# Spilled gates stored by groups of four keys, and stored from the SyncE queue

## The chip, the cores and the metric

The kernel runs on one core of a Trainium2 chip. The metric is the device time of one execution in microseconds (us). The kernel before was timed three times: 1623.45, 1630.87 and 1631.17 us, a median of 1630.87 us. One more execution was profiled.

## The reference, cut to what matters

The program is one decoder block over 512 tokens of width 1024: three gated token mixers, then a product-key expert retrieval ("PEER"). Only the second part matters here. Each token picks 16 of 128 x 128 = 16384 experts for each of 8 heads, 128 (expert, gate) pairs in all, and computes

```python
a   = einsum('cd,ced->ce', h_c, u[e_c])
act = gelu(a) * g_c
out = einsum('ce,ced->cd', act, v[e_c])
```

An expert's number is `e1 * 128 + e2`; the first key `e1` splits the tables u and v into 128 blocks of 128 experts, and the kernel calls the number of such a block a key, `k`.

## The kernel before, in words

The 512 tokens are four blocks of 128. For blocks 0 and 1 the kernel gathers each picked row of u and v from memory by an indirect DMA issued by GpSimd (line 833, tile `row`, 512 KB each): a dot product on VectorE for u (line 843, tile `scr`), a scaled sum on VectorE for v (line 852, tile `mg`). At most five such rows have a buffer, some more for a while, and at most `AHEAD` = 4 are requested ahead of the one in use. `step()` does one row, and JOBS lists all 512 of them.

For blocks 2 and 3 (`DENSE`, `ND` = 2 blocks, `TD` = 256 tokens) it computes all experts densely. For each key k it multiplies 128 expert rows of u with the 256 tokens (`dense_u`, line 971 in full float32, or lines 142 to 144 as three products of split operands), applies gelu, multiplies by a matrix of gates that is zero for the experts not picked, and multiplies with 128 rows of v, summing over keys in four PSUM banks (`dense_v`, lines 142 to 144). One key's activations `ga` are 128 experts x 256 tokens.

The gate matrix is made in the *spread* stage. Its loop over n takes four tokens at a time (`GT` = 4): VectorE builds one-hot sides `o` (line 1026), ScalarE scales one by the gates (line 1029), TensorE multiplies them (line 1041), and the product holds, for the 128 second keys in the partitions, four tokens x 128 first keys. The gates of the first 32 keys (`KEPT`) are multiplied at once into `ga` by VectorE (line 1044). Those of the other 96 keys are copied by ScalarE into three staging tiles `st` (line 1047), each for `SPILT` = 32 keys x `TG` = 32 tokens; the staging tiles take turns with two sets of buffers. When 32 tokens are full, three DMAs (line 1051) write them to the memory tensors `gd`, one for each dense block. There are 8 such groups of tokens, so 24 DMAs of 512 KB, all on ScalarE's DMA queue.

The *last* stage is the loop over k at line 1173. `operands(k)` asks for the v block of key k + 3 on SyncE's queue (`fetch_v`, line 1073, tiles `raw` and `last`), and every fourth key asks for the gates of the next four (`GK` = 4) keys in two DMAs of 256 KB on the same queue (`get_gates`, line 1065, tile `gq`), 48 in all. Then ScalarE splits v into `whi` (line 1090) and the activations into `ah` (line 1088), VectorE makes the remainders `wlo` (line 128) and `al` (line 1093), and multiplies gates in (line 1085). Between these it does the rows of `step()`. The blocks of u still to do (71 of 128) come on ScalarE's queue there (line 935), every second one is split by ScalarE and VectorE into `uhi` and `ulo` (lines 958 and 960).

The order on TensorE, VectorE and GpSimd is the program's order (a manual schedule). ScalarE's and SyncE's instructions are placed by a scheduler that simulates time, with some SyncE issues held in program order. Each engine takes its instructions in order, and a DMA issue that waits holds up what stands behind it on its engine.

Of the kernel before, what the change touches and what calls it, by code (L numbers as in the profile page):

```python
# [7 lines left out]
F32 = mybir.dt.float32  # L8
# [13 lines left out]
NK = 128  # L22
# [5 lines left out]
ND = len(DENSE)  # L28
# [3 lines left out]
SPILT = (128 - KEPT) // 3  # L32
# [14 lines left out]
TG = 32  # L47
GK = 4
# [8 lines left out]
def tile_block(ctx: ExitStack, tc: tile.TileContext, t: dict, out: bass.AP):  # L57
    nc = tc.nc
# [6 lines left out]
    dram = ctx.enter_context(tc.tile_pool(name="dram", bufs=1, space=bass.MemoryType.DRAM))  # L65
# [5 lines left out]
    def bank(tag):  # L71
        return psum.tile([128, 512], F32, tag=tag, name=tag, bufs=BANKS[tag])
# [191 lines left out]
    raw = wp.tile([128, WSLOT], F32, tag="raw", name="raw")  # L264
# [654 lines left out]
    gq, acc, late, v_raw, u_raw = {}, {}, [], {}, {}  # L919
# [55 lines left out]
    f = Found(found, BIG)  # L975
# [21 lines left out]

    cp = build.enter_context(tc.tile_pool(name="cp", bufs=1))
    ctx.enter_context(tc.manual_schedule(engines={mybir.EngineType.Pool, mybir.EngineType.DVE, mybir.EngineType.PE}))
    gd = [dram.tile([128, 128 // TG, NK * TG], F32, name=f"gd{i}") for i in range(ND)]  # L1000


    slots, sides, stage = {}, {}, {}
# [14 lines left out]
    def tokens(n):  # L1018
        i, q = divmod(n, 128 // GT)
        return i, q * GT, slice(q * GT, (q + 1) * GT)  # L1020
# [11 lines left out]
    def spread(n):  # L1032
        i, t0, _ = tokens(n)
        o = sides.pop(n)
        if t0 % TG == 0:

            stage[0] = [wp.tile([128, WSLOT], F32, tag=tag, name="st")[:, :SPILT * TG].rearrange(
                "p (k t) -> p k t", t=TG) for tag in (("whi", "wlo") * 3)[n // (TG // GT) % 2 * 3:][:3]]
        ps = bank(("sc", "tp")[n % 2]).rearrange("p (t k) -> p t k", t=4)
        for u in range(GT):  # L1040
            PE.matmul(ps[:, u], o[:, 1, u], o[:, 0, u], start=True, stop=True)
        c = t0 % TG
        kept = soon[:, :KEPT, i * 128 + t0:i * 128 + t0 + GT]
        V.tensor_mul(kept, ps[:, :, :KEPT].rearrange("p t k -> p k t"), kept)
        for hf in range(3):
            k0 = KEPT + hf * SPILT
            A.copy(stage[0][hf][:, :, c:c + GT], ps[:, :, k0:k0 + SPILT].rearrange("p t k -> p k t"))
        if c + GT == TG:
            for hf in range(3):
                k0 = KEPT + hf * SPILT  # L1050
                nc.scalar.dma_start(gd[i][:, t0 // TG, k0 * TG:(k0 + SPILT) * TG],
                                  stage[0][hf].rearrange("p k t -> p (k t)"))

    def get_gates(k, part):

        k -= k % GK
        if not KEPT <= k < NK or not 0 <= part < GQ_PARTS:
            return
        if part == 0:
            gq["raw"] = gp[0].tile([128, ND, 128 // TG, GK * TG], F32, tag="gq", name="gq")  # L1060
            gq[k] = gq["raw"].rearrange("p i g (k t) -> p (i g) k t", k=GK)
        n = ND * (128 // TG) // GQ_PARTS
        i, g = divmod(part * n, 128 // TG)
        tc.keep_in_program_order(
            nc.sync.dma_start(gq["raw"][:, i, g:g + n], gd[i][:, g:g + n, k * TG:(k + GK) * TG]))

    def fetch_v(k):
        if k < NK:
# [6 lines left out]
    def operands(k):  # L1075

        fetch_v(k + VFAR)
        if k % GK == 0:
            for part in range(GQ_PARTS):
                get_gates(k + GK, part)  # L1080
        raw, a = v_raw.pop(k), ga(k)
        if k >= KEPT:
            m = gq[k - k % GK][:, :, k % GK]
            g = a.rearrange("p (g t) -> p g t", t=TG)
            V.tensor_mul(g, m, g)
        ah = gp[0].tile([128, TD], F32R, tag="ah", name="ah")
        al = gp[0].tile([128, TD], F32R, tag="al", name="al")
        A.copy(ah, a)  # L1088
        hi = wp.tile([128, WSLOT], F32R, tag="whi", name="whi")[:, :D]
        A.copy(hi, raw)  # L1090
        yield
        w = [x[:, 0] for x in rest((raw, hi, 1, 1), 0.0)]
        V.tensor_sub(al, a, ah.bitcast(F32))
        yield w, ah, al
# [39 lines left out]
    for n in range(AHD, NBAT + AHD):  # L1134
        if n < NBAT:
            build_sides(n)
        if n == NBAT - PLAIN_ROWS:
            ahead[0] = AHEAD
        if n == NBAT - V_EARLY:
            for k in range(VFAR):  # L1140
                fetch_v(k)
        credit[0] += STEPS_N
        while credit[0] >= 1.0 and done[0] < known[0]:
            credit[0] -= 1.0
            step()
        if (n + 4) % PER == 0 and n + 4 < NBAT:
            turn_block((n + 4) // PER)
        spread(n - AHD)
        for _ in range(STEPS_U):
            if tile_u is None and FIRST_U + COVER + n * DURING // NBAT >= k_u:  # L1150
                tile_u = dense_u(k_u)
                next(tile_u)
                k_u += 1
            elif tile_u is not None and next(tile_u, 1):
                tile_u = None
# [132 lines left out]
```

## Time and profile before

| | |
|---|---|
| profiled execution | 1625.96 us, span of its instructions 1624.2 us, 26373 instructions |
| busy | PE 1535.0 us, DVE 1406.5 us, ACT 781.2 us, POOL 783.8 us |
| spread stage | about 867 to 1010 us; the 24 writes are issued from 883.0 to 1010.3 us |
| last stage | about 1010 to 1618 us; the 48 reads are issued from 1134.5 to 1582.5 us |
| DMA queues | q0 is GpSimd's, q1 SyncE's, q10 ScalarE's |
| moved in all | 531.85 MB |

PE is TensorE, DVE is VectorE, ACT is ScalarE, POOL is GpSimd, SP is SyncE; SPq and ACTq are DMA issues by SyncE and ScalarE. A row of a group gives line, engine, operation, output tile and input tiles, and count. A row of waits gives who waited at which line, for whom, us in total, how often, and the longest. The DMA share is the mean busy share of the core's 16 DMA engines; it is built from the times of single packets, which overlap a little, so it can pass 1. A packet of a queue is one piece of contiguous memory, or a 4-byte completion note; a DMA over 128 partitions has 16 of the latter, one for each DMA engine, and these are the packets listed under 512 B.

### The profile page before, as it was taken

What the parts mean: (1) busy time and instruction counts of PE and PEld (TensorE: products, weight loads), DVE (VectorE), ACT (ScalarE), POOL (GpSimd) and SP (SyncE); (2) the same over time, 40 slices, a digit from 0 to 9 for tenths busy, and PEclk for the clock granted to TensorE, in tenths of its full rate; (3) what the DMA queues carried; (4) which work ended last, traced back from release to release, by engine and by line L of the source; (5) the groups of instructions that cost most, each with busy time, mean ns of one, the idle gap of its engine ahead of it and who ended that gap; (6) DMA issues with size and microseconds to landing.
All of it is one profiled execution on the core that took longest, in us unless ns stands there. A gap on an engine that the chain in (4) does not pass through costs nothing. (4 is left out here: it accounts for less than half of the span.)

```text
span 1624.2 us, 26373 instructions
## 1 busy us (share of the span) xinstructions
PE 1535.0 (95%) x9030; PEld 1375.9 (85%) x9030; DVE 1406.5 (87%) x2721; ACT 781.2 (48%) x1782; POOL 783.8 (48%) x625
## 2 busy tenths in 40 slices
PE   6999999999998988997999999899999999999998
PEld 5999889988887988987888998788888788787887
DVE  5677458889988999999998999888898899898997
ACT  6787437645445434443116888343343333333332
POOL 1100011757666455588563332656565555555551
PEclk9999999999998999999999999999999999999999
DMA  8587753899998899867997999999999999999995
GB/s 298 180 278 222 247 178 118 301 350 321 344 320 288 301 347 347 303 212 255 339 396 287 364 387 335 394 403 389 399 399 395 392 401 400 400 401 386 398 400 222
DMA packets 177334, 531.85 MB, mean 327 GB/s; under 512 B 17456, under 2 KB 46384, under 8 KB 177200
## 3 DMA queue, kind: packets, MB, share of 16 engines
q0 software_dynamic: 73728, 268.47, 44.4%
q1 hardware_dynamic: 90224, 213.46, 36.5%
q10 hardware_dynamic: 13248, 48.24, 7.6%
q8 instruction: 71, 1.16, 0.3%
q14 instruction: 63, 0.52, 0.1%
HBM read 515.42 MB, written 14.68 MB: 326 GB/s over the span
## 5 line engine op out<-in xcount | busy, mean ns | idle before, releaser
L833 POOL DMA_INDIRECT row<-in_peer_v_dram,eidx x256 | 348.3, 1360 | 280.2 <-DVE mg L852 150.6
L833 POOL DMA_INDIRECT row<-in_peer_u_dram,eidx x256 | 331.7, 1296 | 269.9 <-DVE scr L843 159.4
L128 DVE TENSOR_TENSOR wlo<-raw,whi 128x1024 fp32r<-128x1024 f32 (+1 forms) x243 | 305.8, 1260 | 38.1 <-ACT whi L116 37.0
L843 DVE SCALAR_TENSOR_TENSOR scr<-row,own 128x1024 bf16<-128x1024 f32 x256 | 312.6, 1221 | 29.3 <-DMA row<-in_peer_u_dram,eidx 27.0
L852 DVE SCALAR_TENSOR_TENSOR mg<-row,acts,mg 128x1024 f32<-128x1024 f32 x237 | 303.5, 1281 | 19.1 <-DMA row<-in_peer_v_dram,eidx 16.7
L971 PE MATMUL mm<-h2f,hhi 128*128 128x256 f32 x976 | 222.9, 379 | 0.0
L971 PEld LDWEIGHTS mm<-h2f,hhi 128*128 128x128 f32 x976 | 182.5, 190 | 24.6
L116 ACT CAST whi<-raw 128x1024 fp32r<-128x1024 f32 (+1 forms) x148 | 154.8, 1049 | 88.5 <-PE mm L143 44.2
L189 POOL TENSOR_TENSOR rsy<-rsv,mhalf 128x4 f32<-128x4 f32 (+5 forms) x25 | 38.8, 1553 | 220.4 <-DVE rsv L188 126.5
L1090 ACT CAST whi<-raw 128x1024 fp32r<-128x1024 f32 x96 | 100.5, 1047 | 68.6 <-DMA raw<-in_peer_v_dram 49.6
L1088 ACT CAST ah<-ga 128x256 fp32r<-128x256 f32 x116 | 47.0, 406 | 155.8 <-PE tp L143 107.8
L142 PE MATMUL mm<-hhi,whi 128*128 128x384 f32 x320 | 110.3, 345 | 8.0 <-ACT ga L973 6.7
L143 PE MATMUL mm<-hlo,whi 128*128 128x384 f32 x320 | 110.6, 346 | 0.0
L144 PE MATMUL mm<-hhi,wlo 128*128 128x384 f32 x320 | 109.8, 343 | 0.0
L142 PE MATMUL sc<-whi,ah 128*128 128x512 f32 x256 | 107.3, 419 | 2.4 <-ACT ah L1088 2.2
L142 PE MATMUL mm<-whi,hhi 128*128 128x256 f32 (+1 forms) x360 | 103.9, 290 | 3.2 <-DVE g L572 1.9
L143 PE MATMUL sc<-wlo,ah 128*128 128x512 f32 x256 | 101.1, 395 | 3.8 <-DVE wlo L128 3.8
L143 PE MATMUL mm<-wlo,hhi 128*128 128x256 f32 (+1 forms) x360 | 102.3, 285 | 0.4 <-DVE wlo L128 0.3
L144 PE MATMUL mm<-whi,hlo 128*128 128x256 f32 (+1 forms) x360 | 101.2, 283 | 0.8 <-DVE hlo L629 0.8
L144 PE MATMUL sc<-whi,al 128*128 128x512 f32 x256 | 101.1, 395 | 0.0
L142 PE MATMUL tp<-whi,ah 128*128 128x512 f32 x256 | 100.5, 393 | 0.0
L144 PE MATMUL tp<-whi,al 128*128 128x512 f32 x256 | 100.4, 392 | 0.0
(289 smaller groups left out, 3866.7 us busy)
## 6 DMA issues: line engine op xcount, KB each, us to landing
raw<-in_peer_v_dram SPq DMA_DIRECT2D x96, 512.0 KB, 9.1
hhi<-in_uT_dram ACTq DMA_DIRECT2D x68, 512.0 KB, 7.8
raw<-in_w_tr_dram SPq DMA_DIRECT2D x48, 512.0 KB, 5.1
raw<-in_w_nat_dram SPq DMA_DIRECT2D x40, 512.0 KB, 5.2
last<-in_peer_v_dram SPq DMA_DIRECT2D x32, 512.0 KB, 7.2
hhi<-in_uT_dram SPq DMA_DIRECT2D x28, 512.0 KB, 6.9
raw<-in_w_o_dram SPq DMA_DIRECT2D x24, 512.0 KB, 5.6
hlo<-in_uT_dram SPq DMA_DIRECT2D x24, 512.0 KB, 6.6
```

The lines of the kernel that those rows point to most:

```text
L116: A.copy(hi[:, :n * w], raw[:, :n * w])
L128: V.tensor_sub(lo, raw, hi.bitcast(F32))
L142: PE.matmul(ps, lh, rh, start=first, stop=False)
L143: PE.matmul(ps, lh, rl, start=False, stop=False)
L144: PE.matmul(ps, ll, rh, start=False, stop=last)
L189: G.tensor_tensor(y, v, mhalf[:, :n], op=OP.pow)
L833: G.indirect_dma_start(out=r, out_offset=None, in_=t["peer_" + tab], in_offset=bass.IndirectOffsetOnAxis(ap=eidx[b][:, j:j + 1], axis=0))
L843: V.scalar_tensor_tensor(scr, r, 1.0, h2n[b], op0=OP.mult, op1=OP.mult, accum_out=acts[b][:, c]))
L852: V.scalar_tensor_tensor(x1[b], r, acts[b][:, c], x1[b], op0=OP.mult, op1=OP.add))
L971: PE.matmul(ps[:, :TD], w[:, dc], h2f[dc], start=dc == 0, stop=dc == KC - 1)
L1088: A.copy(ah, a)
L1090: A.copy(hi, raw)
```

## The change

The memory tensor `gd` gets another order. Before, a partition held for each of four groups of 32 tokens all 128 keys, 32 tokens each. Now it holds for each four keys the four groups of tokens, each with 4 x 32 gates. What a read of four keys wants of one dense block, four groups x 4 x 32 gates, is then one piece of 2 KB in each partition, where it was four pieces of 512 bytes. A write of 32 keys x 32 tokens, which was one piece of 4 KB, is now eight pieces of 512 bytes. The writes are issued by SyncE in place of ScalarE. What is computed is the same.

```diff
-    gd = [dram.tile([128, 128 // TG, NK * TG], F32, name=f"gd{i}") for i in range(ND)]
+    gd = [dram.tile([128, NK // GK, 128 // TG, GK * TG], F32, name=f"gd{i}") for i in range(ND)]
...
             for hf in range(3):
                 k0 = KEPT + hf * SPILT
-                nc.scalar.dma_start(gd[i][:, t0 // TG, k0 * TG:(k0 + SPILT) * TG],
-                                  stage[0][hf].rearrange("p k t -> p (k t)"))
+                nc.sync.dma_start(gd[i][:, k0 // GK:(k0 + SPILT) // GK, t0 // TG],
+                                  stage[0][hf].rearrange("p (a k) t -> p a (k t)", k=GK))
...
         tc.keep_in_program_order(
-            nc.sync.dma_start(gq["raw"][:, i, g:g + n], gd[i][:, g:g + n, k * TG:(k + GK) * TG]))
+            nc.sync.dma_start(gq["raw"][:, i, g:g + n].rearrange("p g k -> p (g k)"),
+                              gd[i][:, k // GK, g:g + n].rearrange("p g k -> p (g k)")))
```

The change moves no instruction on PE, DVE and POOL. On SyncE, in the spread stage, the writes come between the loads of u (line 937, `hhi` and `hlo`). Before:

```order
L937 DMA hlo<-in_uT_dram 128x1024 x3
L937 DMA hhi<-in_uT_dram 128x1024 x3
L937 DMA hlo<-in_uT_dram 128x1024 x3
L1167 DMA out_dram<-mg_2246 128x1024
L937 DMA hhi<-in_uT_dram 128x1024 x3
```

Now:

```order
L1051 DMA gd_8904<-st 128x8x128 x3
L937 DMA hlo<-in_uT_dram 128x1024 x3
L1051 DMA gd_8904<-st 128x8x128 x3
L937 DMA hhi<-in_uT_dram 128x1024 x3
L1051 DMA gd_8904<-st 128x8x128 x3
L937 DMA hlo<-in_uT_dram 128x1024 x3
L1168 DMA out_dram<-mg_2246 128x1024
L1051 DMA gd_8904<-st 128x8x128 x3
L937 DMA hhi<-in_uT_dram 128x1024 x3
```

Three writes of 128 x 8 pieces stand ahead of each three loads of u, on the engine that only issues DMAs.

At the end of the spread stage the last writes stand on SyncE between loads of u and of v (`raw`, `last`), just ahead of the last stage. Before:

```order
L1073 DMA raw<-in_peer_v_dram 128x1024
L937 DMA hhi<-in_uT_dram 128x1024
L1073 DMA raw<-in_peer_v_dram 128x1024
L937 DMA hhi<-in_uT_dram 128x1024
L1073 DMA last<-in_peer_v_dram 128x1024
L1073 DMA raw<-in_peer_v_dram 128x1024 x3
```

Now:

```order
L1074 DMA raw<-in_peer_v_dram 128x1024
L937 DMA hhi<-in_uT_dram 128x1024
L1074 DMA raw<-in_peer_v_dram 128x1024
L1051 DMA gd_8905<-st 128x8x128 x3
L937 DMA hhi<-in_uT_dram 128x1024
L1074 DMA last<-in_peer_v_dram 128x1024
L1051 DMA gd_8905<-st 128x8x128 x3
L1074 DMA raw<-in_peer_v_dram 128x1024 x3
```

The seventh group of writes stands ahead of the last load of u on this engine, and the eighth ahead of the fifth block of v. In the last stage the order on SyncE is the same; the shape of the reads changes. Before:

```order
L1073 DMA last<-in_peer_v_dram 128x1024
L1065 DMA gq<-gd_8904 128x4x128
L1065 DMA gq<-gd_8905 128x4x128
L1073 DMA raw<-in_peer_v_dram 128x1024 x3
L1073 DMA last<-in_peer_v_dram 128x1024
```

Now:

```order
L1074 DMA last<-in_peer_v_dram 128x1024
L1065 DMA gq<-gd_8904 128x512
L1065 DMA gq<-gd_8905 128x512
L1074 DMA raw<-in_peer_v_dram 128x1024 x3
L1074 DMA last<-in_peer_v_dram 128x1024
```

A read of four keys of a dense block was 128 x 4 pieces and is 128 pieces. On ScalarE the 24 issues are gone from between the copies, and in the first keys of the last stage one `ah` stands behind a `whi` instead of ahead of it.

## The prediction, on record before the changed kernel ran

> **What bounds the kernel now.** I read the page first, then a table of the stages, then who waits in the last stage, then what the DMA queues do. The page:
>
> ```profile
> span 1624.2 us, 26373 instructions
> PE 1535.0 (95%) x9030; PEld 1375.9 (85%) x9030; DVE 1406.5 (87%) x2721; ACT 781.2 (48%) x1782; POOL 783.8 (48%) x625
> DMA 13%; PE 11%; issue 9%; POOL 5%; DVE 4%; ACT 0%; ACTq 0%; POOLq 0%; DVEq 0%
> ```
>
> PE and DVE are busy nearly throughout, and the chain that ended last is mostly DMA. Both can be true of different stages, so here is the view of windows. Its columns are the stretch, its length, the busy time of PE, PEld, DVE, ACT and POOL, then the granted clock, the DMA share and GB/s. The rows are the spread stage with the writes, the turn to the last stage, the last stage before the gates are read, and the last stage with the reads:
>
> ```profile
> 880.00:1000.00 120.00, 120.00 (x763) 111.26 (x762) 120.00 (x171) 98.17 (x394) 41.83 (x41) 1.00 0.97 366
> 1010.00:1034.00 24.00, 17.16 (x77) 13.49 (x76) 22.23 (x39) 7.06 (x11) 12.63 (x9) 0.93 1.00 389
> 1040.00:1130.00 90.00, 90.00 (x468) 77.86 (x467) 78.54 (x118) 36.68 (x57) 51.89 (x37) 1.00 1.02 401
> 1130.00:1610.00 480.00, 461.68 (x2331) 393.75 (x2330) 433.49 (x559) 184.26 (x285) 262.24 (x178) 1.00 1.02 391
> ```
>
> In the spread stage PE works 120.00 of 120 us, and so does DVE: nothing waits there, and every delay of either would cost its full length. The DMA share is 0.97. In the last stage PE works without a gap (90.00 of 90) until the gates are read; from then on it loses 480 - 461.7 = 18.3 us, with the DMA engines at 1.02, which is as full as this trace gets. So the stage with the reads is the one where DMA time is worth something, and the most that can be won there is some 18 us. The waits from 1130 to 1612 us, of PE, DVE and ACT:
>
> ```profile
> PE mm L144 <- DVE ulo L960: 15.3, 13, 2.6
> PE sc L142 <- ACT ah L1088: 2.2, 1, 2.2
> DVE al L1093 <- ACT ah L1088: 21.7, 12, 3.9
> DVE mg L852 <- DMA row<-in_peer_v_dram,eidx: 14.6, 19, 1.8
> DVE scr L843 <- DMA row<-in_peer_u_dram,eidx: 7.7, 7, 2.1
> ACT whi L1090 <- DMA raw<-in_peer_v_dram: 48.3, 15, 9.1
> ```
>
> PE waits for `ulo`, the remainder of a split block of u, made by DVE. DVE is late because gathered rows land late (14.6 + 7.7 = 22.3 us), or because ACT got its block of v late. One case of each, from the timelines of DVE, of ACT and of PE:
>
> ```profile
> 1154.90 1.23 DVE L843 SCALAR_TENSOR_TENSOR scr<-row,own 128x1024 bf16<-128x1024 f32 x1 [1.98 <-DMA row<-in_peer_u_dram,eidx]
> 1159.62 1.22 DVE L960 TENSOR_TENSOR ulo<-hhi,uhi 128x1024 fp32r<-128x1024 f32 x1
> 1405.34 1.05 ACT L1090 CAST whi<-raw 128x1024 fp32r<-128x1024 f32 x1 [6.47 <-DMA raw<-in_peer_v_dram]
> 1406.73 0.42 DVE L1093 TENSOR_TENSOR al<-ga,ah 128x256 fp32r<-128x256 f32 x1 [2.70 <-ACT ah L1088]
> 1412.66 0.38 PE L144 MATMUL mm<-hlo,ulo 128*128 128x256 f32 x1 [2.62 <-DVE ulo L960]
> ```
>
> **The reads.** These are the DMA views of 1150 to 1590 us (first three rows), of 130 to 140 us (next two), and of 1617 to 1624 us, where the output is written in pieces of 2 KB (last two):
>
> ```profile
> DMA packets 68258, 174.91 MB, mean 398 GB/s; under 512 B 5688, under 2 KB 28475, under 8 KB 68226
> q0 software_dynamic: 24205, 88.15, 50.7%
> q1 hardware_dynamic: 36479, 58.93, 36.4%
> ...
> DMA packets 1463, 2.81 MB, mean 281 GB/s; under 512 B 91, under 2 KB 91, under 8 KB 1463
> q1 hardware_dynamic: 1463, 2.81, 86.9%
> ...
> DMA packets 577, 1.06 MB, mean 151 GB/s; under 512 B 64, under 2 KB 64, under 8 KB 576
> q1 hardware_dynamic: 576, 1.05, 39.5%
> ```
>
> A share is of 16 engines, so 440 us hold 7040 us of engine time. q0 moves rows of 4 KB: 88.15 MB are 21521 pieces, 50.7% is 3569 us, 165.8 ns a piece. q1 moves v in pieces of 4 KB and gates in pieces of 512 bytes; the latter are 28475 - 5688 = 22787 pieces, 11.67 MB. The other 47.26 MB are 11538 pieces at 165.8 ns, 1913 us; of q1's 2563 us 650 are left, **28.5 ns for a piece of 512 bytes**. Four cost 114.0 ns. A straight line between the two sizes gives 87.3 ns for 2 KB. The bounds are rows: 39.5% of 112 us over 512 pieces is 86.4 ns (written, at the quiet end), 86.9% of 160 us over 1463 - 91 = 1372 pieces is 101.3 ns (read, early). I take the line, which lies by the lower one. The reads are 24 times two DMAs of 128 x 4 pieces, 24576 in all, and become 6144. Each saves 26.7 ns: 164 us of engine time, **10.3 us of all 16 engines** (4.9 to 10.6 by the bounds).
>
> The Trainium skill, page "DMA: Bandwidth & Descriptors", section "Why small descriptors are slow (HBM only)", gives each packet a fixed overhead of about three cycles beside one cycle for 32 bytes. By it 512 bytes, 2 KB and 4 KB cost 19, 67 and 131 cycles; scaled to the 165.8 ns above, that is 24.0 and 84.8 ns, and the reads would save, as an estimate, 4.4 us of 16 engines. The row's 28.5 ns disagrees: a small piece costs more here than that overhead.
>
> How much of 10.3 us does PE feel? If the DMA engines alone set the pace of this stretch, all of it. If the reads' 24576 x 28.5 ns, 43.8 us of 16 engines, made PE's 18.3 us of waits and these shrink in proportion (10.3 of 43.8, 24%), it is 4.3 us. The chain of causes runs through rows that miss their moment by 0.9 us in the mean (22.3 us in 26 waits), so neither limit is strict; I take the middle, **-7.3 us**.
>
> **The writes.** The DMA view of 880 to 1000 us, where 21 of the 24 writes are issued, their rows and those of the rows' issues and landings, and SyncE's loads of u:
>
> ```profile
> q10 hardware_dynamic: 3024, 11.01, 24.3%
> hlo<-in_uT_dram SPq DMA_DIRECT2D x9, 512.0 KB, 7.7
> L1051 ACTq DMA_DIRECT2D gd<-st x24: 326/418/1510, 883.0 to 1010.3; - x24
> L833 POOL DMA_INDIRECT row<-in_peer_u_dram,eidx x27: 932/936/1827, 919.5 to 998.4; - x27
> L833 POOL DMA_INDIRECT row<-in_peer_v_dram,eidx x14: 933/936/1827, 880.2 to 917.0; - x14
> DMA to landing us min/median/max: 4.2/7.9/11.6
> 903.79 11.70 SPq L937 DMA_DIRECT2D hhi<-in_uT_dram  x3
> ```
>
> q10 holds the writes alone: 11.01 MB are 2688 pieces of 4 KB in 24.3% of 1920 us, 173.6 ns each; all 3072 take 533 us. The change makes them 24576 pieces of 512 bytes. No row shows such a write. Below, eight cannot cost less than the one they replace: 21.7 ns, nothing added. Above, one cannot cost more than a written 2 KB piece: 86.4 ns, 99 us of 16 engines. I take the read's 28.5 ns, since writes and reads of 4 KB differ by 5% only: 700 us, **10.4 us of 16 engines more**, 9.1 of them in these 120 us. Room there, by the fullest steady share: (1.02 - 0.97) x 120 = 6.0 us. So the stage ends some 3.1 us behind in DMA work. What hides that is work asked for early. 41 rows in 120 us are one in 2.9 us, six ahead 17 us, at the end four ahead 11.7 us, against a landing of 7.9 + 3.1 us. Loads of u are issued about 5.7 us apart (three in 11.70) into a ring of six, a lead of some 28 us against 7.7 + 3.1. I put **+1.0 us** (0 to 3.1) there. Without the cover all 10.4 us would be paid, since PE has no gap.
>
> **The queue.** ACT loses 24 issues of 418 ns, 10 us, and works 98 of 120 us there without PE ever waiting: nothing. SP now waits for the staging copies, with three loads of u and at most a block of v queued behind; their lead covers it. Last come the eighth group and the turn of the stages, from ACT's timeline:
>
> ```profile
> 1019.85 1.05 ACT L1090 CAST whi<-raw 128x1024 fp32r<-128x1024 f32 x1 [0.60 <-DMA gd<-st]
> 1022.26 0.41 ACT L1088 CAST ah<-ga 128x256 fp32r<-128x256 f32 x1 [1.36 <-DVE scr L843]
> ```
>
> `whi` shares its buffers with the staging tiles, so this one waits until a write has landed. Three writes take an engine 3 x 64 x 28.5 ns = 5.5 us instead of 3 x 8 x 173.6 ns = 4.2, and stand behind one or two 1.3 us shares of loads on SP's queue: 1.3 to 3.9 us later, less the 1.36 us that ACT waits right after. **+1.0 us** (0 to 2.5).
>
> **Sum.** 1625.96 - 7.3 + 1.0 + 1.0 = **1620.7 us**, 0.33% under the profiled execution. That one lies 4.9 us under the median shown (1630.87) and 2.5 over the lowest; I compare like with like.
>
> **The rivals.** *The stalls go altogether.* Before the reads start, the same rows and blocks meet a DMA share of 1.02 and PE loses nothing; so the stage is near a threshold, and a little less traffic may be enough. Against it: three quarters of the reads' engine time stays. 1625.96 - 18.3 + 2.0 = 1609.7 us.
>
> *Nothing comes back.* The waits are set by the ring of rows: four ahead, and the time from issue to landing hardly moves. The DMA views of 1040 to 1130 us (first row) and of 1130 to 1600 us give its median last:
>
> ```profile
> row<-in_peer_u_dram,eidx POOLq DMA_INDIRECT x37, 8.8
> ...
> row<-in_peer_v_dram,eidx POOLq DMA_INDIRECT x128, 9.4
> row<-in_peer_u_dram,eidx POOLq DMA_INDIRECT x50, 10.1
> ```
>
> All the reads' traffic added 0.6 to 1.3 us to a landing, so a quarter of it is 0.2 to 0.3 us. Against: the waits are no longer than that by much. 1626 to 1628 us.
>
> *The spread stage becomes DMA-bound, and the kernel slower.* Place: 880 to 1010 us, PE and DVE without a gap. At x ns a written piece the writes add (24576 x - 533 us) / 16, of which 6.9 us (6.0 x 24/21) find room. The loss passes 0.5% in all once 14.4 us are over, that is from x = 35.6 ns on, a quarter above the read. At 40 ns, 28.1 us are added, 21.2 over: 1625.96 - 7.3 + 1.0 + 21.2 = 1640.9 us. For it: no written piece of this size is in the trace, and the share is already 0.97. Against: written pieces of 4 and 2 KB cost what read ones do.
>
> **Chances and range.** Something under 0.5%, 8 us, can't be told from no change here. Forecast 0.42 (1614 to 1627 us; 0.10 of it faster, 0.32 same); stalls gone 0.23, faster; nothing comes back 0.13, same; spread stage bound 0.22, of which 0.20 slower and 0.02 same. Together 0.33 faster, 0.47 same, 0.20 slower. The range reaches from the second case to the last: 1609 to 1640 us.
>
> **What would show it.** Right: the written pieces near 28.5 ns and the read ones near 87; PE still at 120 of 120 in the spread stage; PE's waits for `ulo` after the reads begin down from 15.3 to some 8 us; fewer and shorter waits of DVE for rows. Wrong: PE or DVE gaps between 880 and 1010 us, ACT waiting for a write to land before a staging copy, or `ulo` waits as long as before.

## The result, and the profile after

The changed kernel takes 1618.69 us (median of 17 runs, 1613.4 to 1624.41), the kernel before beside it 1627.63 us (17 runs, 1620.74 to 1635.58). The ratio is 0.995, with a 95% interval from 0.9936 to 0.9964: some 8 us less, and the interval lies across the bound of 0.5%. The profiled execution of the changed kernel took 1613.45 us, 5.2 us under its own median. So its span overstates the gain, and what follows reads stages and waits rather than ends. The page after:

```profile
span 1611.6 us, 26380 instructions
PE 1532.9 (95%) x9030; PEld 1377.0 (85%) x9030; DVE 1406.2 (87%) x2721; ACT 782.9 (49%) x1782; POOL 780.6 (48%) x625
```

Where did the 12.6 us between the two spans arise? The view of one source line gives the first and last start of its instructions. The first matmul of the spread stage and the last sums of the program, before:

```profile
L1041 PE MATMUL sc<-o x256: 272/275/347, 863.1 to 1005.7; 128*128 128x128 f32 x128
L1196 DVE TENSOR_TENSOR mg<-mg,sc x2: 686/688/689, 1617.9 to 1618.6; 128x512 f32<-128x512 f32 x2
```

and after (line numbers from 1066 on are one higher there):

```profile
L1041 PE MATMUL sc<-o x256: 272/275/347, 859.1 to 1001.8; 128*128 128x128 f32 x128
L1197 DVE TENSOR_TENSOR mg<-mg,sc x2: 687/688/689, 1605.6 to 1606.3; 128x512 f32<-128x512 f32 x2
```

4.0 us were there before the spread stage began, in instructions that the change does not touch; they are scatter of single executions (over the profiles of all runs this first start lies between 859.1 and 865.8 us). The spread stage takes as long as it did (142.6 us from first to last start, now 142.7). The last stage is 8.4 us shorter (from 1005.7 to 1617.9, now 1001.8 to 1605.6). The spread stage and the last stage before the gates are read, in the view of windows after:

```profile
880.00:1000.00 120.00, 120.00 (x764) 111.35 (x763) 119.84 (x174) 100.58 (x395) 40.00 (x41) 1.00 1.04 371
1040.00:1130.00 90.00, 90.00 (x468) 77.69 (x467) 80.08 (x119) 36.09 (x56) 53.22 (x37) 1.00 1.01 393
```

PE still has no gap in either, though the DMA share in the spread stage went from 0.97 to 1.04. The waits from 1130 to 1612 us are:

```profile
PE mm L144 <- DVE ulo L960: 10.4, 13, 1.5
PE sc L143 <- DVE wlo L128: 0.6, 1, 0.6
DVE mg L852 <- DMA row<-in_peer_v_dram,eidx: 16.8, 22, 2.0
DVE al L1094 <- ACT ah L1089: 11.0, 9, 3.0
DVE scr L843 <- DMA row<-in_peer_u_dram,eidx: 8.0, 8, 2.0
ACT whi L1091 <- DMA raw<-in_peer_v_dram: 2.2, 1, 2.2
```

PE waits 11.0 us where it waited 18.0 (the prediction's two rows, 15.3 + 2.2, and 0.5 for `wlo`). But the waits for gathered rows did not shrink: 16.8 + 8.0 = 24.8 us against 22.3. What went is ACT's wait for its block of v, 48.3 to 2.2 us, and with it half of VectorE's wait for `ah`, 21.7 to 11.0. The times from issue to landing say the same. From the DMA views of 1130 to 1600 us, first the two rows of before, then four of after:

```profile
raw<-in_peer_v_dram SPq DMA_DIRECT2D x73, 512.0 KB, 10.4
gq<-gd SPq DMA_DIRECT2D x48, 256.0 KB, 13.3
```

```profile
raw<-in_peer_v_dram SPq DMA_DIRECT2D x72, 512.0 KB, 8.4
gq<-gd SPq DMA_DIRECT2D x48, 256.0 KB, 10.2
row<-in_peer_v_dram,eidx POOLq DMA_INDIRECT x128, 9.7
row<-in_peer_u_dram,eidx POOLq DMA_INDIRECT x49, 9.8
```

The gates and the blocks of v behind them on SyncE's queue land 3.1 and 2.0 us sooner; rows land as before (9.4 and 10.1).

7.0 us of waits are less than the 8.4 us by which the last stage is shorter. The granted clock accounts for most of the rest. Before, one of PE's longest waits is followed by a stretch in which the clock drops; first PE's row, then the window around it:

```profile
1530.94 0.38 PE L144 MATMUL mm<-hlo,ulo 128*128 128x256 f32 x1 [2.32 <-DVE ulo L960]
1530.00:1535.00 5.00, 4.06 (x21) 4.06 (x22) 4.96 (x6) 0.41 (x1) 2.24 (x3) 0.66 1.06 374
```

From 1531.16 us on PE starts 17 matmuls in 3.53 us; at the 0.12 us apart at which it starts the next ones they would take 2.0, so some 1.5 us are lost. The changed kernel has no such drop between 1040 and 1600 us; its longest wait there is 1.5 us. The profiles of all the runs show eleven such drops between 1130 and 1600 us, each right behind a wait of PE of 1.9 us or more; not every wait of that length has one. So a long wait can cost more than its length.

**The prices.** The DMA view of 1150 to 1590 us after:

```profile
q0 software_dynamic: 24642, 89.71, 51.2%
q1 hardware_dynamic: 19990, 60.72, 34.9%
gq<-gd SPq DMA_DIRECT2D x46, 256.0 KB, 10.3
```

q0's pieces of 4 KB are 21902 in 3604 us, 164.6 ns each. The 46 reads are 5888 pieces of 2 KB, 12.06 MB; the other 48.66 MB of q1 are 11880 pieces, 1955 us at q0's price; of q1's 2457 us 502 are left, **85.2 ns** a piece. And the view of 880 to 1000 us, the writes:

```profile
DMA packets 31012, 44.50 MB, mean 371 GB/s; under 512 B 1358, under 2 KB 22862, under 8 KB 31000
q1 hardware_dynamic: 25152, 23.07, 56.1%
q0 software_dynamic: 5848, 21.28, 47.1%
```

q0's 5195 pieces of 4 KB take 904 us, 174.1 ns each. The written pieces are 22862 - 1358 = 21504, 11.01 MB; the other 12.06 MB of q1 are 2944 pieces of 4 KB, 512 us; of q1's 1077 us 565 are left, **26.3 ns** a written piece. The same working on a second profile of the changed kernel (it comes below) gives 28.2 ns for a written piece and 82.8 for a piece of 2 KB, so these prices are good to some 2 ns.

### The profile page after: what moved, and what is told of

It reads as the page before. It is cut to its first block, busy times and chain, and to the rows that moved or that the text cites. A ratio compares the mean times of both kernels' runs of the same rounds, so it can differ in the third digit from the quotient of the medians.

```text
span 1611.6 us, 26380 instructions
## 1 busy us (share of the span) xinstructions
PE 1532.9 (95%) x9030; PEld 1377.0 (85%) x9030; DVE 1406.2 (87%) x2721; ACT 782.9 (49%) x1782; POOL 780.6 (48%) x625
## 4 chain that ended last, share of the span: by engine, by line
PE 36%; DVE 22%; DMA 17%; issue 15%; POOL 7%; ACT 2%; SPq 0%; DVEq 0%; POOLq 0%; ACTq 0%
DMA row<-in_peer_u_dram,eidx 8%; DMA row<-in_peer_v_dram,eidx 7%; POOL row L833 6%; PE mm L143 6%; PE mm L144 6%; PE mm L142 6%; DVE mg L852 6%; DVE o L1026 3%; DVE scr L843 3%; PE mm L971 3%; DVE wlo L128 2%; PE mm L295 2%; PE sc L142 1%; PE sc L143 1%; PE sc L144 1%
## 5 line engine op out<-in xcount | busy, mean ns | idle before, releaser
L973 ACT ACTIVATE ga<-mm 128x256 f32<-128x256 f32 x84 | 31.7, 379 | 143.5 <-PE mm L971 143.4
```

## The experiments

Two theories stood at the start. **The engines' time:** TensorE's waits in the last stage follow how much time the 16 DMA engines spend, and the reads in larger pieces cost them less. **The late v:** only what stands behind the reads on SyncE's queue counts; they land sooner, and with them v. A third question was which part of the change costs something. Differences are given against the kernel before unless "the change" is named. Each ratio has its interval behind it; in all runs the kernel before was timed on the same chip.

### The queue alone, and the layout alone

Old layout, writes issued by SyncE:

```diff
-                nc.scalar.dma_start(gd[i][:, t0 // TG, k0 * TG:(k0 + SPILT) * TG],
+                nc.sync.dma_start(gd[i][:, t0 // TG, k0 * TG:(k0 + SPILT) * TG],
```

> The old layout (written pieces of 4 KB, read pieces of 512 bytes), with the 24 writes issued by SyncE instead of ScalarE. Theory A (engine time: the gain is the time that the 16 DMA engines save on the read pieces, 10.3 us, of which PE feels most) and theory B (late v: the gain comes from blocks of v that stand behind the gates' reads on SyncE's queue and land too late; less time for the reads brings them in time, and the gathered rows are no better off) both expect no change, ratio 0.998 to 1.002, since neither the reads nor the order of reads and v changes. If the engine that issues the writes matters by itself, this run shows it: 10 us of issue leave ScalarE, so a ratio under 0.997 would say that the gain is there. With pieces of 4 KB SyncE should need about 0.4 us for each issue, and not the 5 to 6 us for three that the changed kernel shows.

Measured 1.0012 [0.9993, 1.0031]: the queue alone changes nothing that can be measured. The layout alone is the change with its writes issued by ScalarE:

```diff
-                nc.sync.dma_start(gd[i][:, k0 // GK:(k0 + SPILT) // GK, t0 // TG],
+                nc.scalar.dma_start(gd[i][:, k0 // GK:(k0 + SPILT) // GK, t0 // TG],
```

> The new layout, with the 24 writes left on ScalarE. In the changed kernel SyncE is held 3 to 6 us by each group of three writes of 1024 pieces. If that is a property of the DMA and not of SyncE, ScalarE is held as long, 8 times some 5 us = 40 us in a stage of 150 us in which it works about 125 us, and PE, which had no gap there, gets gaps: the spread stage 10 to 25 us longer, and with the 8 us gained in the last stage a ratio of 1.002 to 1.012. If ScalarE hides it, the ratio is that of the change, 0.995, and SyncE was not needed.

Measured 1.0015 [0.9985, 1.0044], where the change has 0.995: the gain is gone. The writes' own rows, of the old layout on SyncE, of the changed kernel, and of this one on ScalarE, each of its own profile (duration of an issue in ns, least, median and longest; first and last start). Below the last stand PE's waits for `o` and the window of the spread stage with ScalarE's writes:

```profile
L1051 SPq DMA_DIRECT2D gd<-st x24: 326/440/2087, 883.0 to 1010.2; - x24
```

```profile
L1051 SPq DMA_DIRECT2D gd<-st x24: 377/623/5690, 879.0 to 1006.3; - x24
```

```profile
L1051 ACTq DMA_DIRECT2D gd<-st x24: 366/540/6799, 880.5 to 1016.6; - x24
PE tp L1041 <- ACT o L1029: 4.6, 3, 3.0
880.00:1000.00 120.00, 116.69 (x724) 107.33 (x723) 115.59 (x164) 89.46 (x372) 38.97 (x39) 0.99 1.01 353
```

An issue of 1024 pieces of 512 bytes can hold the engine that issues it for 5.7 to 6.8 us. SyncE has nothing else to do. ScalarE has: the one-hot sides that it scales (`o`) come late, PE waits for them, and the stretch from the first write to the last is 136.1 us in place of 127.3. In the last stage PE waits as little as in the change (10.1 us for `ulo`). This profiled execution is a mild one: it took 1618.55 us, where the executions of this kernel ran from 1618.11 to 1645.72. Its spread stage is 6.0 us longer than the change's (148.7 us from first to last start); what the longer executions lost beyond that no profile shows. So the queue is worth nothing by itself and 0.0065 of 1627 us, some 10.6 us, with this layout. The Trainium skill, page "DMA: Bandwidth & Descriptors", section "Issuing engines are not separate DMA queues", says that starting DMAs from several engines at once saves only the sequencer's time for it, "usually small relative to the DMA itself". The runs agree that this time is what counts, and here it was not small: issues of up to 6.8 us, where a write lands after 9.8 us in the median of the changed kernel.

### The reads alone

Writes as before (4 KB, by ScalarE); the reads fetch 2 KB in one piece, which here are not the gates that belong there:

```diff
-            nc.sync.dma_start(gq["raw"][:, i, g:g + n], gd[i][:, g:g + n, k * TG:(k + GK) * TG]))
+            nc.sync.dma_start(gq["raw"][:, i, g:g + n].rearrange("p g k -> p (g k)"),
+                              gd[i][:, k // GK % 4, KEPT * TG + (k - KEPT) // GK // 4 * 512:KEPT * TG + (k - KEPT) // GK // 4 * 512 + 512]))
```

> The old layout and the old writes (4 KB, by ScalarE), but each read of four keys takes 2 KB in one piece from another place of the same memory, so that wrong gates are read: the gain of the read pieces without the price of the written ones. Both theories expect the last stage as in the changed kernel (PE's waits from the reads on some 11 us instead of 18), so a ratio of 0.994 to 0.996; if the written pieces of 512 bytes cost anything in the time, it is by that much lower than the 0.995 of the change.

Measured 0.9965 [0.9948, 0.9982]. PE's waits fall as in the change, the waits for rows do not (25.7 us):

```profile
PE mm L144 <- DVE ulo L960: 10.5, 13, 1.3
DVE mg L852 <- DMA row<-in_peer_v_dram,eidx: 16.3, 21, 1.8
DVE scr L843 <- DMA row<-in_peer_u_dram,eidx: 9.4, 12, 2.1
```

The change, which pays for its writes too, is no slower than this. So the writes in 512 bytes cost nothing that can be measured, as long as SyncE issues them.

### Is it the order on SyncE's queue?

The old layout, with the reads (512 bytes) issued by ScalarE, so that no v stands behind them:

```diff
-            nc.sync.dma_start(gq["raw"][:, i, g:g + n], gd[i][:, g:g + n, k * TG:(k + GK) * TG]))
+            nc.scalar.dma_start(gq["raw"][:, i, g:g + n], gd[i][:, g:g + n, k * TG:(k + GK) * TG]))
```

> The old layout and writes, with the 48 reads of 512-byte pieces issued by ScalarE, so that no block of v stands behind them on SyncE's queue (blocks of u on ScalarE's queue do). Engine time is the same as before. Theory A: no change, ratio 0.998 to 1.002. Theory B: ScalarE's 48 us of waits for v go, and PE's waits fall from 18 to some 11 us: ratio 0.994 to 0.997, less whatever ScalarE loses by 48 issues of about 0.6 us and by u landing later.

Measured 1.0063 [1.0037, 1.0089]: slower. The waits for v are gone, but now the block of u (`hhi`), which stands behind the reads on ScalarE's queue, comes late. PE waits longer at a time, up to 4.5 us, and five drops of the clock follow (0.98 in the mean from 1130 to 1600 us, 1.00 before):

```profile
PE mm L144 <- DVE ulo L960: 21.8, 15, 4.5
PE sc L143 <- DVE wlo L128: 2.7, 1, 2.7
DVE ga L1085 <- DMA gq<-gd: 7.7, 3, 3.9
ACT uhi L958 <- DMA hhi<-in_uT_dram: 34.1, 9, 6.8
```

A milder form keeps both reads on SyncE's queue, but asks for them at two keys, with a block of v between:

```diff
-        if k % GK == 0:
-            for part in range(GQ_PARTS):
-                get_gates(k + GK, part)
+        if k % GK < GQ_PARTS:
+            get_gates(k + GK, k % GK)
```

> The kernel before (512-byte pieces read, 4 KB written by ScalarE), with the two reads of four keys not one behind the other on SyncE's queue but one at each of two keys, with a block of v between them. Engine time, pieces and bytes are those of before; only the longest stretch of reads ahead of a block of v is halved. If the change's gain comes from engine time, no change: ratio 0.998 to 1.002, and ScalarE waits for v as before (48 us). If it comes from blocks of v that stood too long behind the reads, ScalarE's waits for v fall below 15 us, DVE's waits for ScalarE from 21.7 to some 11 us, and the ratio is 0.994 to 0.998. The second read is asked for three keys ahead, some 14 us, and landed in 13 before: if it comes late, VectorE waits for gq.

Measured 1.0009 [0.9992, 1.0026]. Half as much stands ahead of a v, and yet:

```profile
PE mm L144 <- DVE ulo L960: 15.4, 15, 2.5
DVE ga L1084 <- DMA gq<-gd: 13.8, 9, 2.8
DVE mg L852 <- DMA row<-in_peer_v_dram,eidx: 6.0, 10, 1.1
DVE scr L843 <- DMA row<-in_peer_u_dram,eidx: 4.8, 7, 1.4
ACT whi L1089 <- DMA raw<-in_peer_v_dram: 52.3, 25, 6.6
```

The waits for rows halve (10.8 us), the gates themselves now come late (13.8), v waits as long in more and shorter pieces, and PE loses what it lost. The late v as a matter of order finds no support: with the same pieces, where the lateness shows depends on the order, and how much of it reaches PE does not get less. Neither run took v's lateness away without making something else late, so v's own part in PE's waits is not shown apart.

### Take the reads away, or join two

The old layout, with 46 of the 48 reads left out (all later keys take the first gates in place of their own):

```diff
+        if k > KEPT:
+            gq[k] = gq[KEPT]
+            return
```

> The kernel before, with the gates of four keys read once and used for all 96 keys (46 of 48 reads left out, wrong gates): the whole price of the reads. They take some 44 us of the 16 engines. If PE's 18 us of waits after 1130 us all come from the reads, as the prediction's second rival has it, they go to 0 to 4 us and the ratio is 0.989 to 0.991. If a good part of them comes from gathered rows that land late anyway (theory B: DVE's 22 us of waits for rows did not change with the change), PE keeps about 10 us of waits for ulo, and the ratio is that of the change, 0.994 to 0.996.

Measured 0.987 [0.9841, 0.9899], some 21 us. From 1130 on PE waits 1.9 us in two waits:

```profile
PE mm L144 <- DVE ulo L960: 1.9, 2, 1.0
1130.00:1600.00 470.00, 467.95 (x2394) 402.48 (x2393) 440.69 (x571) 187.58 (x290) 268.77 (x179) 1.00 0.97 378
```

46/48 of 43.8 us of engine time, 42 us, went, and 16 of PE's 18 us of waits went with it; the DMA share is 0.97, below what it is when the reads run. So the reads' traffic makes all but 2 us of those waits. The next step would be one read of 4 KB for both dense blocks, the change with the two blocks side by side in memory (the writes go to their half of it, and the reads of four keys are one part in place of two, `GQ_PARTS = 1`):

```diff
-    gd = [dram.tile([128, NK // GK, 128 // TG, GK * TG], F32, name=f"gd{i}") for i in range(ND)]
+    gd = dram.tile([128, NK // GK, ND * (128 // TG), GK * TG], F32, name="gd")
...
-            nc.sync.dma_start(gq["raw"][:, i, g:g + n].rearrange("p g k -> p (g k)"),
-                              gd[i][:, k // GK, g:g + n].rearrange("p g k -> p (g k)")))
+            nc.sync.dma_start(gq["raw"].rearrange("p i g k -> p (i g k)"),
+                              gd[:, k // GK].rearrange("p g k -> p (g k)")))
```

> The changed kernel with the two dense blocks' gates side by side in memory, so that four keys are one DMA of 128 pieces of 4 KB instead of two of 128 pieces of 2 KB; the writes stay pieces of 512 bytes. Engine time for the reads falls from 6144 x 87 to 3072 x 166 ns, 1.5 us of 16 engines, and 24 DMAs with 16 completion notes each go. Theory A: 1 to 2 us below the change, ratio 0.993 to 0.995. Theory B: one DMA instead of two stands ahead of the next v, whose landing gets shorter again, and the little that v still costs goes: also 0.993 to 0.995, with ScalarE's waits for v at 0 to 2 us. Either way it should not be slower than the change.

Measured 0.9955 [0.9938, 0.9972], the change again. By the prices above, two pieces of 85.2 ns become one of some 165, which saves 6 ns a pair, 1 us of 16 engines in all. Its profiled execution took 1620.26 us, and PE waited 14.7 us for `ulo` in it. If nothing but that 1 us is different, the waits of one execution scatter by about 4 us. The changed kernel itself, run once more unchanged, gave:

> The changed kernel once more, on the chip and in the rounds of the next run and of the reads apart. 0.993 to 0.997 by every theory.

0.9946 [0.9925, 0.9967], with 10.7 us for `ulo`, in an execution of 1616.21 us. PE's waits after 1130 us are, in the three profiles with old reads in their old place or apart (before, SyncE alone, reads apart), 18.0, 17.4 and 16.5 us; in five with larger pieces (the change twice, its writes on ScalarE, the reads alone, one read) 11.0, 10.9, 10.3, 10.7 and 14.9 us. The means differ by 5.7 us, and no value of the one group falls into the other.

### How near the writes are to costing something

The change, and each write a second time into a memory tensor that nobody reads:

```diff
-    gd = [dram.tile([128, NK // GK, 128 // TG, GK * TG], F32, name=f"gd{i}") for i in range(ND)]
+    gd, gx = ([dram.tile([128, NK // GK, 128 // TG, GK * TG], F32, name=f"{n}{i}") for i in range(ND)] for n in ("gd", "gx"))
...
-                nc.sync.dma_start(gd[i][:, k0 // GK:(k0 + SPILT) // GK, t0 // TG],
-                                  stage[0][hf].rearrange("p (a k) t -> p a (k t)", k=GK))
+                for to in (gd, gx):
+                    nc.sync.dma_start(to[i][:, k0 // GK:(k0 + SPILT) // GK, t0 // TG],
+                                      stage[0][hf].rearrange("p (a k) t -> p a (k t)", k=GK))
```

> The changed kernel with every group of gates written a second time, in the same pieces of 512 bytes, to a memory tensor that nobody reads. The first copy cost nothing that the spread stage shows. The second adds 24576 x 27.5 ns = 676 us of engine time, 42 us of 16 engines, to a stage of 130 us whose DMA share is 1.04 already: if DMA time was only just covered, the stage gets 30 to 45 us longer and the ratio is 1.013 to 1.022. If pieces of 512 bytes are cheap because they fill gaps of the engines, the stage grows by less than 15 us and the ratio stays under 1.005.

Measured 1.0163 [1.0133, 1.0192], 0.0213 or some 35 us above the change:

```profile
880.00:1000.00 120.00, 107.60 (x652) 98.00 (x651) 102.77 (x143) 78.91 (x317) 36.47 (x36) 0.94 1.04 360
L1052 SPq DMA_DIRECT2D gd<-st x24: 377/1444/9776, 882.3 to 1045.7; - x24
ACT st L1047 <- DMA gx<-st: 30.3, 8, 6.1
```

At 26.3 ns the copies are 24576 x 26.3 / 16 = 40.4 us of 16 engines. So the stage had room for only a small part of them: the staging tiles are still being written out when ACT wants them again, and PE stands. How large that part was can't be had from the difference of some 6 us, since the granted clock is 0.94 in this window too, and the loss holds that as well. The DMA share is 1.04 with the second copy as it is without: the change already stands at what this stage was seen to carry.

### Can the waits that are left be ordered away?

In the last stage VectorE does, key by key, rows of blocks 0 and 1 ahead of the split of u. The first of two tries moves that split ahead of the rows (this diff is against the change):

```diff
-        while done[0] < min(len(JOBS), start + (len(JOBS) - start) * (k + 1) // (NK - 4)):
-            step()
-        ready = next(coming) if coming else None
         for u, n in us:
...
             k_u += 1
+        while done[0] < min(len(JOBS), start + (len(JOBS) - start) * (k + 1) // (NK - 4)):
+            step()
+        ready = next(coming) if coming else None
         dense_v(k, *now)
```

> The changed kernel with the split of the next block of u (uhi, ulo) put ahead of the gathered rows of a key in the program, where it stood behind them; TensorE's order is the same. If what is left of PE's waits is ulo standing behind rows that land late, as the waits in the changed kernel say (10.4 us, 13 times), these waits go to under 3 us and the ratio to before is 0.987 to 0.991. If PE is held by the DMA engines' total time instead, it waits for something else as long (wlo, or a block of u that has not landed) and the ratio stays at 0.994 to 0.996.

Measured 0.9924 [0.9895, 0.9953], and once more:

> The changed kernel with the split of u ahead of the rows once more. It was at 0.992 (0.990 to 0.995), the change at 0.995 (0.994 to 0.996) elsewhere. If the gain of taking ulo from behind the rows is real, it is again 2 to 5 us below the run of the change beside it; if it only moved the wait to wlo at the same price, the two medians agree within 2 us.

0.9929 [0.9907, 0.9952]; its median is 1615.97 us, that of the change beside it 1618.05. The waits for `ulo` are gone and others have come. The only row of PE in the first of the two profiles:

```profile
PE sc L143 <- DVE wlo L128: 9.2, 10, 1.7
```

The second try moves `ready = next(coming)`, the gates' step of the next key, ahead of the rows as well, so that rows come last in a key (against the first try):

```diff
+        ready = next(coming) if coming else None
         while done[0] < min(len(JOBS), start + (len(JOBS) - start) * (k + 1) // (NK - 4)):
             step()
-        ready = next(coming) if coming else None
         dense_v(k, *now)
```

> The changed kernel with the split of u ahead of the rows (as in the run before) and, in addition, the gates' step of the next key ahead of the rows of this one, so that in each key the work that waits for the rows stands last on VectorE. Nothing is left out. Theory of the one line on VectorE (the rows that come late stand ahead of TensorE's operands there, and carry the lateness of the memory to TensorE): TensorE's waits for ulo and wlo in the last stage, 9 us in the run before, come under 3 us, and the time to 0.986 to 0.990 of the kernel before. Theory of the engines' time (the traffic is the same, so the lateness only moves to what is now last): TensorE's waits stay at 7 us or more in sum, under other names (al behind ah, v, or the ring of rows that is held longer), and the ratio stays at 0.992 to 0.994 or is worse.

Measured 0.9936 [0.9916, 0.9956]:

```profile
PE mm L144 <- DVE ulo L960: 7.3, 12, 1.7
PE sc L143 <- DVE wlo L128: 0.6, 3, 0.2
```

The theory of the one line on VectorE expected under 3 us and 0.986 to 0.990; 7.9 us and 0.9936 are what the engines' time expected. A likely reason, which no run isolates, is that what comes last in one key stands ahead of something in the next. The three readings of the reordered kernels (0.9924, 0.9929, 0.9936) all lie below the three of the change and of the one read (0.995, 0.9946, 0.9955), by some 3 us in the mean (0.0021); the intervals overlap, so a small gain is likely and not settled.

## Why the prediction was right, and where not

Predicted were 1620.7 us, 5.3 less than the profiled execution of the kernel before; measured were 1618.69 us in the median, and by the ratio 8 us less (5.9 to 10.4). The forecast case came, a little larger than drawn. Its steps:

- **Pieces.** Written 28.5 ns forecast, 26.3 and 28.2 measured; read 87.3 forecast, 85.2 and 82.8 measured. The price of a write, for which the trace before had no row, was rightly taken from the read of the same size. The reads save (24576 x 28.5 - 6144 x 85.2) / 16 = 11.1 us (10.3 forecast), the writes cost (24576 x 26.3 - 533) / 16 = 7.1 us, or 10.0 at 28.2 ns (10.4 forecast).
- **What PE feels of the reads.** Forecast -7.3 us, the middle between 4.3 and 10.3. Measured: 18.0 to 11.0 us of waits, -7.0, in the two profiles, -5.7 over the groups of profiles. The size was right, and in part by luck: the prediction gave two limits and no reason for the point between them.
- **The way it reaches PE.** This step failed: "The chain of causes runs through rows that miss their moment", with "fewer and shorter waits of DVE for rows" as its sign. The rows' landing and waits stayed; v and the gates came sooner. In its place the runs show no single transfer as the channel. Rows' waits may halve (reads apart), and v's waits may vanish (reads on ScalarE), while PE waits about as long or longer. PE's waits fell where the engines' time fell; reordering took at most some 3 us more off them (7.9 to 9.5 us against 11.0 and 10.9).
- **The spread stage.** Forecast +1.0 us, measured 0.1. In the second profile of the change the stage took 144.3 us, 1.6 more, but there the granted clock is 0.66 from 860 to 865 us, ahead of the first write. The added 7.1 to 10.0 us of engine time found cover, though the room was forecast as 6.9 for the whole stage, from a fullest share of 1.02; the changed kernel ran this stretch at 1.04. So the room was drawn too small. The doubled writes show that it ends; its size stays open.
- **The queue.** That ACT's 24 issues are worth nothing holds for the old layout (1.0012). The step priced them at 418 ns each, the row of 4 KB pieces. It missed that with 1024 pieces an issue lasts up to 6.8 us, which on ScalarE would have cost the whole gain. The forecast did not suffer, since SyncE has that time.
- **The turn of the stages.** Forecast: ACT's `whi` 1.3 to 3.9 us later, +1.0 us in the end. Two rows of the changed kernel, of ACT's timeline and of PE's waits from 1003 to 1040 us:

```profile
1015.14 1.05 ACT L1091 CAST whi<-last 128x1024 fp32r<-128x1024 f32 x1 [4.39 <-DMA gd<-st]
PE mm L144 <- DVE ulo L960: 4.4, 1, 4.4
```

  The wait for the write went from 0.60 to 4.39 us, +3.8, the top of the range. The pieces have little part in it: with pieces of 4 KB issued by SyncE (the queue alone) the row is

```profile
ACT whi L1090 <- DMA gd<-st: 4.0, 1, 4.0
```

  But PE's wait at that place rose only from the 3.5 us in this row of before:

```profile
PE mm L144 <- DVE ulo L960: 3.5, 1, 3.5
```

  With PE's `wlo` waits there, which fell from 3.3 to 2.9 us, it is +0.5. Even that can't be put down to the change: where ScalarE writes 4 KB and this wait is 0.6 us (the reads alone), PE waits 4.3 + 3.3 = 7.6 us there, more than the 7.3 of the changed kernel.
- **Sum.** -7.0 + 0.1 + 0.5 = -6.4 us of the 8.4 by which the last stage and the turn are shorter and of the 8 by the ratio. The clock's drop in the profile before, 1.5 us, is most of what is left: a price of long waits that the prediction's sum does not hold. It differs from one execution to the next; the change's second profile has one such drop.

Of the rivals, **the stalls go altogether** had its premise right, since without the reads nearly all waits are gone, and its threshold wrong: a quarter less engine time took away a third to 39% of them. **Nothing comes back** saw that the rows' landing would hardly move, and was wrong that this sets PE's waits. **The spread stage becomes DMA-bound** needed 35.6 ns a written piece; there were 26.3 to 28.2. The doubled writes show that its mechanism is real. The Trainium skill's overhead of three cycles a packet ("DMA: Bandwidth & Descriptors", "Why small descriptors are slow (HBM only)") gave, as an estimate, 24.0 ns for 512 bytes and 84.8 for 2 KB. The written pieces (26.3 to 28.2) cost more than that, as the read ones did (28.5); the 2 KB pieces (85.2 and 82.8) agree with it.

## What to carry to other kernels

Where the DMA engines are full, price each transfer in engine time by the piece, move small pieces from the stage that has no room to one that has, and expect only a part of the engine time back (here half to two thirds). A wait that the profile shows for one late transfer is a symptom there: reordering queues or instructions mostly moved it to the next in line here, while less engine time shrank the sum. Look for the longest waits of TensorE as well as their sum, since a drop of its clock can follow them. Put transfers of many small pieces on an engine that only issues, since an issue can hold its engine for microseconds.

## What the runs showed of the hardware that was not expected

- One DMA issue of 1024 pieces of 512 bytes held its engine for up to 5.7 us on SyncE and 6.8 us on ScalarE, up to 9.8 us where the writes were doubled. With 128 pieces of 4 KB the longest issue took 2.1 us on SyncE. The medians stay at 540 to 623 ns in the single ones, so it is not a fixed price per piece; what makes some of them long was not tried.
- A written piece of 512 bytes costs the DMA engines 26.3 to 28.2 ns, no more than a read one (28.5), and a piece of 2 KB 85.2 ns, half of 4 KB. Joining pieces paid from 512 bytes to 2 KB (114.0 ns against 85.2 for the same bytes) and hardly from 2 to 4 KB (170.4 against 164.6).
- TensorE's granted clock can drop for a few us right behind a long wait: 0.66 over the 5 us from 1530 us in the kernel before, behind a wait of 2.32 us, with matmuls of `mm` at 0.41 us each in place of 0.28. Another wait of 2.62 us in the same execution (at 1412.66 us) had no drop behind it; what decides is not shown.
